# A product split over the chunks, a scaling moved to ScalarE, and additions moved from GpSimd to VectorE in a one-core decoder step

## The chip, the cores and the metric

The kernel runs on one core of a Trainium2 chip. The time is device microseconds of that core. Below, PE is the matrix engine TensorE (PEld its weight loads), DVE is VectorE, ACT is ScalarE, POOL is GpSimd, SP is SyncE, which issues transfers. PSUM is the memory that matrix products are summed in.

## The reference

One step of a decoder layer over 1032 tokens: a prompt of 1024 and 8 single sample tokens. All operands are float32.

```
h = rmsnorm(x)
u, v, z, xBC, dt = split(h @ w_in)             # one product, columns by part
a = u * (tril(W_s) @ layernorm(v) + b)         # gated mixing inside chunks of 128 tokens
xBC = silu(causal_conv(xBC, width 4));  dt = softplus(dt + bias)
y = ssd_chunked(x, dt, A, B, C)                # state-space scan, decays exp(dt * A)
x = x + concat(a, gated_norm(y, z)) @ w_out
k, v = rmsnorm(mem) @ w_k, w_v                 # 256 memory tokens, 4 heads
x = x + softmax((rmsnorm(x) @ w_q) k^T) v @ w_o
x = x + (silu(n @ w_gate) * (n @ w_up)) @ w_down,  n = rmsnorm(x)
return rmsnorm(x), the states and caches
```

## The kernel before

**Tiles.** Activations lie transposed: 128 features on the partitions, tokens along the row. The tokens go in three chunks, `CH = (0, 512), (512, 768), (768, 1032)`, so a product over one chunk has 512, 256 or 264 columns; `X[0]`, `X[1]`, `X[2]` are the scaled input of the three. Each weight panel is a 128x1024 tile. Every large product is made in three passes for precision: each operand is split into a high part (a cast by ACT, lines 145 and 274, tiles `wh`, `xh`, `fw`, `sP`) and the remainder (a subtraction by DVE or POOL, lines 146 and 275, tiles `wl`, `xl`), and PE adds high·high, high·low and low·high (`mm3`, line 169).

**Order.** One core, six queues; each engine runs its instructions in order. The order is made when the kernel is built, by a scheduler that walks the program and puts the instructions of the engines into their queues by a model of their times. Two other things set it: program order, and `later(n, work)`, which puts a piece of work into the program when `n` further matmuls have been issued (`mm3` counts them).

```
def later(n, work):
    queue.append([n, work])
```

**PSUM.** Products take a buffer from one of two pools: `gbank` (3 buffers, tiles named `g_...`) and `mbank` (5 buffers, `m_...`). A product whose pool has no free buffer waits for an evacuation.

**Stages in order.** Memory keys and values (`g_k`, `g_v`); scaling of the input into `X` (DVE line 383 writes `xtmp`, ACT casts `xh`, DVE or POOL subtracts `xl`); the dt product (lines 461 to 465, tiles `g_dt`), 16 columns of `w_in` split into `wd`, each chunk's 16 matmuls in a buffer of `gbank`; its transposes (`m_dtt`) and the decays (lines 505 to 569); the product that gives x, B and C (`xbc`, 8 panels, evacuated by `conv`, lines 586 to 596: ACT copies `cr` and writes `XS`, DVE adds the taps); the scan and the mixing; the queries (`qa`, `qb`); the attention, in which `scores` (line 1024) makes `ex`, `probs` transposes it (`m_pt`, split to `pTh` and `pTl`) and `pv` multiplies by the values (`m_pv`); the output projections `xoa` and `xob`, whose evacuation `norm_evac` (line 906 and on) adds to the residual `H`, squares it (`n3sq`, ACT) and sums the squares (`n3acc`, line 914); and the gate and up products.

**The gate.** Panels are multiplied in seven products a pair (P1 to P7, tiles `gX`, `gY`, `gZ`, `uX` ...), the sums and differences of two raw panels `fr` being made first (`ws`, lines 1227 to 1230, four of 128x512 a pair), then split into `fw`. The items `n` = 0, 1, 2, ... are gate and up in turn: the first two for one half of the columns alone (256 wide), the next two for both (256 and 264 wide). The norm before it ends late: for each chunk the sums of `n3acc` go through a product with ones (`m_csn`), a square root on ACT (`rsbn`), a few tiny DVE operations (`rsan`, `crvn`), and a product (`m_crn`) whose result scales `H` into `B` (DVE line 1174), which is then split into `sP`.

## Time and profile before

| | us |
|---|---|
| median of 3 runs | 1447.44 (1444.37 to 1452.41) |
| profiled execution, own time | 1451.7 |
| its span, first to last instruction | 1449.9 |
| PE busy | 1384.5 (95%) |
| DVE busy | 991.1 (68%) |
| ACT busy | 609.1 (42%) |
| POOL busy | 426.8 (29%) |

The profiled execution lies near the upper end of the runs. PE is busy almost throughout, so the places that matter are those where it waits (65 us of idle time in all) or runs at a lower granted clock: the row of the page that shows the clock in 40 slices of 36 us stands at 9 or below its full mark in all slices, and only windows of a few us show where it falls. The granted clock is given as a share of full speed: 1.00 is 2.4 GHz, 0.50 is 1.2 GHz, and a value between is a mixture of the two over the window.

### The profile page before, as it was taken

The page shows a single profiled execution, that of the slowest core. Times are in us where ns is not written, and L with a number is a line of the kernel's source. Part 1 is how long each engine was busy: PE and PEld are TensorE (multiplying, and loading weights), DVE is VectorE, ACT ScalarE, POOL GpSimd, SP SyncE. Part 2 cuts the span into 40 slices and gives each one's busy share as a digit, 9 for nine tenths or more (in the row PEclk, how much of TensorE's full clock was granted, in tenths as well). Part 3 has the DMA queues.
Part 4 walks back from the last instruction along what each step waited for, and adds up shares of the span by engine and source line. Part 5 has one row for each costly group of instructions (what it writes and reads, how often), then busy time and mean ns, then how long its engine had stood idle before and what let it go on. Part 6 is the DMA issues. An engine that isn't in the chain of part 4 may idle for free. (4 is left out here: it accounts for less than half of the span.)

```text
span 1449.9 us, 26101 instructions
## 1 busy us (share of the span) xinstructions
PE 1384.5 (95%) x10291; PEld 1313.1 (91%) x10291; DVE 991.1 (68%) x2018; ACT 609.1 (42%) x1103; POOL 426.8 (29%) x324
## 2 busy tenths in 40 slices
...
GB/s 292 195 60 60 61 145 114 99 60 36 217 162 74 175 268 285 88 271 250 148 88 129 169 141 149 118 126 168 154 157 212 169 181 302 222 178 165 204 195 131
DMA packets 145531, 232.67 MB, mean 160 GB/s; under 512 B 8328, under 2 KB 91880, under 8 KB 145024
## 3 DMA queue, kind: packets, MB, share of 16 engines
...
q10 hardware_dynamic: 144, 0.05, 0.0%
...
## 5 line engine op out<-in xcount | busy, mean ns | idle before, releaser
L275 DVE TENSOR_TENSOR fw<-ws,fw 128x512 fp32r<-128x512 f32 x96 | 90.0, 939 | 45.0 <-ACT fw L274 44.7
L145 ACT CAST wh<-wr 128x1024 fp32r<-128x1024 f32 (+1 forms) x85 | 87.9, 1037 | 75.5 <-PE g_gv L169 25.1
L274 ACT CAST fw<-ws 128x512 fp32r<-128x512 f32 x96 | 59.0, 619 | 137.7 <-POOL ws L1228 66.9
L146 POOL TENSOR_TENSOR wl<-wr,wh 128x1024 fp32r<-128x1024 f32 (+1 forms) x30 | 72.6, 2420 | 118.1 <-ACT wh L145 70.2
L1227 POOL TENSOR_TENSOR ws<-fr 128x512 f32<-128x512 f32 x24 | 35.9, 1498 | 210.7 <-DMA fr<-in_w_gate_dram 110.7
L146 DVE TENSOR_TENSOR wl<-wr,wh 128x1024 fp32r<-128x1024 f32 x55 | 71.1, 1295 | 24.7 <-ACT wh L145 24.6
L274 ACT CAST fw<-fr 128x512 fp32r<-128x512 f32 x72 | 44.4, 618 | 82.8 <-PE m_gY L169 20.6
L275 DVE TENSOR_TENSOR fw<-fr,fw 128x512 fp32r<-128x512 f32 x72 | 63.3, 879 | 8.3 <-ACT fw L274 7.9
L275 DVE TENSOR_TENSOR xP<-xsP,xP 128x512 fp32r<-128x512 f32 (+2 forms) x84 | 54.2, 686 | 14.9 <-ACT xP L274 13.4
L1532 PE MATMUL m_d<-xP,dwhi 128*128 128x264 f32 x448 | 64.1, 285 | 0.0
L275 DVE TENSOR_TENSOR dwlo<-dw,dwhi 128x1024 fp32r<-128x1024 f32 x32 | 39.8, 1244 | 34.0 <-ACT dwhi L274 33.9
L1532 PE MATMUL g_d<-xP,dwhi 128*128 128x256 f32 x448 | 63.0, 283 | 0.0
L169 PE MATMUL g_gY<-sP,fw 128*128 128x256 f32 (+1 forms) x432 | 59.1, 286 | 3.8 <-DVE t L1282 2.1
L169 PE MATMUL m_uY<-sP,fw 128*128 128x264 f32 (+1 forms) x432 | 58.5, 284 | 1.9 <-DVE fw L275 1.5
L169 PEld LDWEIGHTS g_gY<-sP,fw 128*128 128x128 f32 x432 | 54.9, 192 | 4.6 <-DVE t L1282 2.6
L1532 PEld LDWEIGHTS m_d<-xP,dwhi 128*128 128x128 f32 x448 | 58.5, 189 | 0.0
L1532 PEld LDWEIGHTS g_d<-xP,dwhi 128*128 128x128 f32 x448 | 57.7, 191 | 0.0
L169 PEld LDWEIGHTS m_uY<-sP,fw 128*128 128x128 f32 x432 | 54.6, 189 | 2.6 <-DVE fw L275 1.7
L274 ACT CAST xP<-xsP 128x512 fp32r<-128x512 f32 (+2 forms) x84 | 45.2, 588 | 27.2 <-DMA xsP<-x_d 17.4
L169 PE MATMUL m_gY<-sP,fw 128*128 128x264 f32 x360 | 49.4, 286 | 5.6 <-DVE t L1282 4.9
L274 ACT CAST dwhi<-dw 128x1024 fp32r<-128x1024 f32 x32 | 33.6, 1050 | 45.9 <-PE m_d L1532 36.4
L169 PEld LDWEIGHTS m_gY<-sP,fw 128*128 128x128 f32 x360 | 45.5, 188 | 7.1 <-DVE t L1282 6.1
(514 smaller groups left out, 3961.0 us busy)
## 6 DMA issues: line engine op xcount, KB each, us to landing
...
```

The source lines that it names most:

```text
L145: nc.scalar.copy(hi[:, s], r[:, s])
L146: (nc.gpsimd if i == 0 or P_QA <= i < P_XO[1] or P_XO[1] <= i < P_XO[1] + 8 and i % 2 else nc.vector).tensor_tensor(lo[:, s], r[:, s], f(h ...
L169: ins = nc.tensor.matmul(ps, lhs(k)[a], rhs(k)[b], start=(fresh and i == 0), stop=(i == n - 1), skip_group_check=not (fresh and done))
L274: nc.scalar.copy(dst_hi, src)
L275: (eng or nc.vector).tensor_tensor(dst_lo, src, f(dst_hi), op=ALU.subtract)
L1227: nc.gpsimd.tensor_tensor(s1, a21, a22, op=ALU.add)
L1532: nc.tensor.matmul(ps[:, : WQ[q]], wdn[n](k)[a], x_at(nm, q, k)[b], start=(i == 0), stop=(i == 3 * NPAIR - 1))
```

## The change

It has three parts. The dt product becomes a function `dt_product(ci)` of one chunk, in a buffer of `mbank`; it is called for the first chunk ahead of the x, B, C product, and for the other two, and for the decays, with `later`, 64, 100 and 120 matmuls into that product. In `scores` the exponentials are scaled by the reciprocal of their sum on ACT where it was DVE. And three pieces of GpSimd's work go to DVE: the remainders of every other panel of the second output projection's weights (4 of 128x1024), the sums of squares before the gate for panels 1 to 5 in each chunk (15 additions), and the panel sums of the first four gate and up items (16 of 128x512).

```diff
+LAG_D = (64, 100, 120)
...
-            (nc.gpsimd if i == 0 or P_QA <= i < P_XO[1] or P_XO[1] <= i < P_XO[1] + 8 and i % 2 else nc.vector).tensor_tensor(lo[:, s], r[:, s], f(hi[:, s]), op=ALU.subtract)
+            (nc.gpsimd if i == 0 or P_QA <= i < P_XO[1] else nc.vector).tensor_tensor(lo[:, s], r[:, s], f(hi[:, s]), op=ALU.subtract)
...
-        for ci in range(3):
-            w = CH[ci][1] - CH[ci][0]
-            ps = gbank(f"dt{ci}")
-            for i in range(16):
-                nc.tensor.matmul(ps[0:16, :w], wd[:, i % 8, :], X[ci](i % 8)[i // 8], start=(i == 0), stop=(i == 15))
-            nc.scalar.copy(dT[:, CH[ci][0] : CH[ci][1]], ps[0:16, :w])
...
+        def dt_product(ci):
+            w = CH[ci][1] - CH[ci][0]
+            ps = mbank(f"dt{ci}")
+            for i in range(16):
+                nc.tensor.matmul(ps[0:16, :w], wd[:, i % 8, :], X[ci](i % 8)[i // 8], start=(i == 0), stop=(i == 15))
+            nc.scalar.copy(dT[:, CH[ci][0] : CH[ci][1]], ps[0:16, :w])
+
+        def decays():
...
+        dt_product(0)
+        for n, work in zip(LAG_D, (lambda: dt_product(1), lambda: dt_product(2), decays)):
+            later(n, work)
         stage(plan_of(P_XBC, 8), X, conv, name="xbc")
...
-                    eng = nc.gpsimd if j < 6 else nc.vector
+                    eng = nc.gpsimd if j < 6 and nm == "n1" else nc.vector
...
-            nc.vector.tensor_scalar(ex[:, 0, :], ex[:, 0, :], sm[:, 0:1], None, op0=ALU.mult)
+            nc.scalar.activation(ex[:, 0, :], ex[:, 0, :], AF.Copy, scale=sm[:, 0:1])
...
             if nm == "P6":
+                eng = nc.vector if n < 4 else nc.gpsimd
                 s1, s2, s3, s4 = wsum[n] = [n3.tile([P, 512], F32, tag="ws", bufs=4, name=f"ws{n}_{i}") for i in range(4)]
-                nc.gpsimd.tensor_tensor(s1, a21, a22, op=ALU.add)
+                eng.tensor_tensor(s1, a21, a22, op=ALU.add)
```

The body of `decays` is what stood in lines 505 to 569, unchanged. In the pieces of order below, a name ends in the number of its tile (one number is one tile), the shape is that of the result, and x4 stands for four instructions of that kind in a row. The lines of the kernel after the change have numbers up to ten higher.

The first place is PE's queue around the dt product. Before, all 48 matmuls of the three chunks stand ahead of the first `g_xbc`; these are the last of them and what follows:

```order
L464 MATMUL g_dt_978<-xl_0_660,wd 16x256 x4
L464 MATMUL g_dt_978<-xl_1_661,wd 16x256 x4
L464 MATMUL g_dt_996<-xh_0_740,wd 16x264 x4
L464 MATMUL g_dt_996<-xh_1_741,wd 16x264 x4
L464 MATMUL g_dt_996<-xl_0_742,wd 16x264 x4
L464 MATMUL g_dt_996<-xl_1_743,wd 16x264 x4
L278 MATMUL m_dtt<-ident,dT 128x16 x4
L169 MATMUL g_xbc_0_1132<-xh_0_513,wh_885 128x512 x4
L169 MATMUL g_xbc_0_1132<-xh_1_514,wh_885 128x512 x4
L169 MATMUL g_xbc_0_1132<-xl_0_515,wh_885 128x512 x4
```

Here `g_xbc`, though it needs only the first chunk's `xh_0` and `xl_0`, comes after the third chunk's dt product, which needs `xh_2` and `xl_2` (written `xh_0_740` to `xl_1_743`). After the change the same place reads:

```order
L516 MATMUL m_dt_1006<-xl_1_516,wd 16x512 x4
L170 MATMUL g_xbc_0_1036<-xh_0_513,wh_885 128x512 x4
L170 MATMUL g_xbc_0_1036<-xh_1_514,wh_885 128x512 x4
L170 MATMUL g_xbc_0_1036<-xl_0_515,wh_885 128x512 x4
L170 MATMUL g_xbc_0_1036<-xl_1_516,wh_885 128x512 x4
L170 MATMUL g_xbc_0_1036<-xh_0_513,wl_886 128x512 x4
L170 MATMUL g_xbc_0_1036<-xh_1_514,wl_886 128x512 x4
L170 MATMUL g_xbc_0_1069<-xh_0_513,wh_1024 128x512 x4
...
L170 MATMUL g_xbc_1_1102<-xl_1_661,wh_885 128x256 x4
L516 MATMUL m_dt_1119<-xh_0_658,wd 16x256 x4
L516 MATMUL m_dt_1119<-xh_1_659,wd 16x256 x4
```

The first chunk's dt product is now followed at once by x, B, C for the first chunk of two panels (`g_xbc_0_1036` and `g_xbc_0_1069`); the second chunk's, `m_dt_1119`, has moved inside the first `g_xbc` of that chunk, and the third chunk's in the same way into the third.

The second place is the gate's beginning. In PE's queue before, from the first item's product P5 on, the norm products of the last two token parts (`m_csn_7853`, `m_crn_7891`, and earlier `m_csn_7725`, `m_crn_7762`) are spread between the first item's products:

```order
L169 MATMUL g_gZ_0_7967<-sP_7292,fw_7824 128x256 x10
L169 MATMUL g_gX_0_7830<-sP_7299,fw_7807 128x256 x2
L235 MATMUL m_csn_7853<-ones,n3acc_7358 128x1 x3
L169 MATMUL g_gX_0_7830<-sP_7299,fw_7807 128x256 x10
L169 MATMUL g_gZ_0_7967<-sP_7292,fw_7824 128x256 x2
L169 MATMUL g_gY_0_7880<-sP_7303,fw_7821 128x256 x12
L169 MATMUL g_gY_0_7880<-sP_7307,fw_7827 128x256 x12
L169 MATMUL g_gZ_0_7967<-sP3h_7310,fw_7844 128x256 x4
L169 MATMUL g_gZ_0_7967<-sP3l_7311,fw_7844 128x256 x4
L169 MATMUL g_gZ_0_7967<-sP3h_7310,fw_7844 128x256 x4
L278 MATMUL m_crn_0_7891<-ident,crvn_7857 128x128 x3
L169 MATMUL m_uX_0_8022<-sP_7288,fw_7877 128x256 x12
```

Between `m_csn_7853` and `m_crn_7891` stand 48 matmuls there. After the change PE's queue has, at the same place:

```order
L170 MATMUL g_gX_0_7830<-sP_7299,fw_7807 128x256 x12
L170 MATMUL g_gZ_0_7967<-sP_7292,fw_7824 128x256 x12
L236 MATMUL m_csn_7725<-ones,n3acc_7250 128x1 x2
L170 MATMUL g_gY_0_7880<-sP_7303,fw_7821 128x256 x12
L170 MATMUL g_gY_0_7880<-sP_7307,fw_7827 128x256 x12
L170 MATMUL g_gZ_0_7967<-sP3h_7310,fw_7844 128x256 x4
L170 MATMUL g_gZ_0_7967<-sP3l_7311,fw_7844 128x256 x4
L170 MATMUL g_gZ_0_7967<-sP3h_7310,fw_7844 128x256 x4
L279 MATMUL m_crn_0_7762<-ident,crvn_7728 128x128 x2
L236 MATMUL m_csn_7853<-ones,n3acc_7358 128x1 x3
L279 MATMUL m_crn_0_7891<-ident,crvn_7857 128x128 x3
L170 MATMUL m_uX_0_8022<-sP_7288,fw_7877 128x256 x12
```

Three of the four norm products have moved behind all of the first item's products, one directly behind another, ahead of the first up product `m_uX`. DVE's queue after the change holds this between `m_crn_7762`, which its first `B` row reads, and `crvn_7857`, which `m_crn_7891` reads:

```order
L276 TENSOR_TENSOR fw_7981<-ws_2_7958,fw_7981 128x512
L1183 SCALAR_TENSOR_TENSOR B_7765<-H_0_7004,vecT,m_crn_0_7762 128x256 x4
L1183 SCALAR_TENSOR_TENSOR B_7771<-H_1_7005,vecT,m_crn_0_7762 128x256 x4
L276 TENSOR_TENSOR fw_8019<-fr_1_7848,fw_8019 128x512
L220 TENSOR_SCALAR rsan_7858<-m_csn_7853 128x3
L221 RECIPROCAL crvn_7857<-rsbn_7859 128x3
L276 TENSOR_TENSOR sP_7906<-B_7765,sP_7905 128x1056
L222 TENSOR_TENSOR rsan_7858<-rsan_7858,crvn_7857 128x3
L223 TENSOR_TENSOR rsan_7858<-rsan_7858,rsbn_7859 128x3
L224 RECIPROCAL crvn_7857<-rsan_7858 128x3
```

The last operation of the norm's chain has moved behind the eight `B` rows, `fw_8019` and `sP_7906`. ACT's queue after the change, from the first `rsbn` on:

```order
L219 ACTIVATE rsbn_7730<-m_csn_7725,eps 128x2
L275 CAST fw_7964<-ws_1_7957 128x512
L275 CAST fw_7998<-ws_0_7956 128x512
L275 CAST fw_7981<-ws_2_7958 128x512
L275 CAST fw_8019<-fr_1_7848 128x512
L1302 ACT_TABLE_LOAD
L1302 ACTIVATE g_0_7799<-g_0_7799 128x2x256
L219 ACT_TABLE_LOAD
L219 ACTIVATE rsbn_7859<-m_csn_7853,eps 128x3
L1308 ACT_TABLE_LOAD
L1308 ACTIVATE g_0_7799<-g_0_7799 128x256
L275 CAST sP_7905<-B_7765 128x1056
```

The square root `rsbn` and the `Silu` of the gate now alternate, with a table load (`ACT_TABLE_LOAD`) at each turn, where before both `rsbn` stood ahead of the first `Silu` with one load; in the whole program the loads go from 29 to 35. The last row, `sP_7905`, is what `sP_7906` on DVE subtracts.

The third place is the attention. DVE's queue at its beginning before, with the scaling of `ex` in it (line 1030) among the reciprocals (`sm`) and the multiplications of the sample tokens' keys (`kc`):

```order
L1020 RECIPROCAL sm_0_5222<-sm_0_5222 128x1
L1030 TENSOR_SCALAR ex_0_5220<-ex_0_5220,sm_0_5222 128x256
L1020 RECIPROCAL sm_0_5253<-sm_0_5253 128x1
L1030 TENSOR_SCALAR ex_0_5251<-ex_0_5251,sm_0_5253 128x256
L1017 TENSOR_REDUCE mx_1_5297<-m_sc_1_5289 128x1
L991 SCALAR_TENSOR_TENSOR kc_0_5187,sdec<-kc_0_5187,qb_5185 128x256 x4
L991 SCALAR_TENSOR_TENSOR kc_1_5189,sdec<-kc_1_5189,qb_5185 128x256 x4
L1020 RECIPROCAL sm_1_5298<-sm_1_5298 128x1
L991 SCALAR_TENSOR_TENSOR kc_0_5193,sdec<-kc_0_5193,qb_5191 128x256 x4
L275 TENSOR_TENSOR pTl_0_5212<-m_pt_0_5304,pTh_0_5211 128x2x128
L991 SCALAR_TENSOR_TENSOR kc_1_5195,sdec<-kc_1_5195,qb_5191 128x256 x4
L1030 TENSOR_SCALAR ex_1_5296<-ex_1_5296,sm_1_5298 128x256
```

After the change DVE's queue there is:

```order
L1029 RECIPROCAL sm_0_5222<-sm_0_5222 128x1
L1029 RECIPROCAL sm_0_5253<-sm_0_5253 128x1
L1026 TENSOR_REDUCE mx_1_5297<-m_sc_1_5289 128x1
L1000 SCALAR_TENSOR_TENSOR kc_0_5187,sdec<-kc_0_5187,qb_5185 128x256 x4
L1000 SCALAR_TENSOR_TENSOR kc_1_5189,sdec<-kc_1_5189,qb_5185 128x256 x4
L1029 RECIPROCAL sm_1_5298<-sm_1_5298 128x1
L1000 SCALAR_TENSOR_TENSOR kc_0_5193,sdec<-kc_0_5193,qb_5191 128x256 x4
L1000 SCALAR_TENSOR_TENSOR kc_1_5195,sdec<-kc_1_5195,qb_5191 128x256 x4
L276 TENSOR_TENSOR pTl_0_5212<-m_pt_0_5304,pTh_0_5211 128x2x128
L1026 TENSOR_REDUCE mx_1_5355<-m_sc_1_5347 128x1
L276 TENSOR_TENSOR pTl_0_5212<-m_pt_0_5362,pTh_0_5211 128x2x128
L1029 RECIPROCAL sm_1_5356<-sm_1_5356 128x1
```

The scaling is gone from it. It stands in ACT's queue, as line 1039:

```order
L275 CAST pTh_0_5211<-m_pt_0_5304 128x2x128
L972 ACTIVATE Q_0_4856<-g_qa_0_5271 128x512
L1039 ACTIVATE ex_1_5296<-ex_1_5296,sm_1_5298 128x256
L275 CAST pTh_0_5211<-m_pt_0_5362 128x2x128
L1028 ACTIVATE ex_1_5354,sm_1_5356<-m_sc_1_5347,mx_1_5355 128x256
L1039 ACTIVATE ex_1_5354<-ex_1_5354,sm_1_5356 128x256
```

There `ex_1_5296` is scaled ahead of the next cast `pTh` and the next exponential, and needs `sm_1_5298`, which on DVE stands behind eight `kc` rows.

## Rows read from the trace of the kernel before

**Rows 1.** The page, part 1: busy us, share of the span, instructions.

```profile
PE 1384.5 (95%) x10291; PEld 1313.1 (91%) x10291; DVE 991.1 (68%) x2018; ACT 609.1 (42%) x1103; POOL 426.8 (29%) x324
```

**Rows 2.** PE's timeline, 70 to 100 us: start us, us, what.

```profile
71.22 0.63 PE L464 MATMUL g_dt<-xh,wd 128*16 128x256 f32 x4
...
87.00 2.90 PE L169 MATMUL g_xbc<-xh,wh 128*128 128x512 f32 x8
...
94.31 1.98 PE L169 MATMUL g_xbc<-xh,wh 128*128 128x512 f32 x8
...
99.75 0.52 PE L169 MATMUL g_xbc<-xh,wh 128*128 128x256 f32 x3
```

**Rows 3.** PE's waits, 60 to 112 us: total us, times, longest us.

```profile
PE g_dt L464 <- ACT xh L274: 6.6, 9, 3.0
```

**Rows 4.** Windows: length, busy PE, PEld, DVE, ACT, POOL, granted clock, DMA share, GB/s.

```profile
76.00:87.00 11.00, 7.81 (x30) 3.36 (x30) 7.59 (x19) 4.63 (x13) 5.29 (x7) 0.50 0.39 111
87.00:98.00 11.00, 11.00 (x47) 8.55 (x47) 4.57 (x16) 4.26 (x6) 0.00 (x0) 0.92 0.00 0
```

**Rows 5.** ACT's timeline, 70 to 108 us.

```profile
83.91 0.41 ACT L274 CAST xh<-xtmp 128x264 fp32r<-128x264 f32 x1 [0.51 <-DVE xtmp L383]
...
94.51 0.59 ACT L586 COPY cr<-g_xbc 128x512 f32<-128x512 f32 x1 [0.28 <-PE g_xbc L169]
95.00 0.79 ACT L587 ACTIVATE XS<-g_xbc,vecT 128x512 f32<-128x512 f32 x1
```

**Rows 6.** Line 1030 by itself: count, min/median/max ns, first and last start.

```profile
L1030 DVE TENSOR_SCALAR ex<-ex,sm x32: 332/354/2493, 514.5 to 670.4; 128x256 f32<-128x256 f32 x32
```

**Rows 7.** Line 419 by itself, the like operation on ACT.

```profile
L419 ACT ACTIVATE vt<-g_v,mrs x8: 461/467/475, 45.6 to 70.9; 128x256 f32<-128x256 f32 x8
```

**Rows 8.** DVE's timeline, 572 to 580 us.

```profile
576.96 2.49 DVE L1030 TENSOR_SCALAR ex<-ex,sm 128x256 f32<-128x256 f32 x1
```

**Rows 9.** POOL's timeline, 572 to 580 us.

```profile
576.92 2.38 POOL L146 TENSOR_TENSOR wl<-wr,wh 128x1024 fp32r<-128x1024 f32 x1 [0.67 <-ACT wh L145]
```

**Rows 10.** PE's waits, 500 to 690 us.

```profile
PE m_sc L169 <- DVE pTl L275: 3.7, 1, 3.7
PE m_pt L278 <- DVE sm L1020: 2.2, 1, 2.2
...
PE m_pt L278 <- DVE ex L1030: 1.7, 2, 1.3
```

**Rows 11.** Windows of the attention, DVE's densest stretch.

```profile
520.00:560.00 40.00, 36.71 (x190) 30.70 (x189) 36.10 (x145) 13.13 (x31) 10.97 (x5) 0.96 0.86 313
```

**Rows 12.** Windows from the output projection into the gate.

```profile
685.00:735.50 50.50, 48.14 (x396) 47.42 (x395) 42.39 (x59) 21.91 (x35) 29.98 (x20) 1.00 0.37 118
735.50:759.00 23.50, 20.64 (x149) 20.17 (x148) 21.90 (x47) 12.53 (x23) 7.66 (x4) 0.85 0.36 112
759.00:798.00 39.00, 34.22 (x275) 33.15 (x274) 38.73 (x51) 16.60 (x29) 17.20 (x10) 1.00 0.39 134
```

**Rows 13.** PE's waits, 685 to 798 us.

```profile
PE g_gY L169 <- DVE t L1282: 2.1, 1, 2.1
...
PE m_csn L235 <- DVE n3acc L914: 1.3, 1, 1.3
```

**Rows 14.** Line 275 by itself, 690 to 798 us.

```profile
L275 DVE TENSOR_TENSOR fw<-ws,fw x16: 672/686/1787, 734.0 to 796.1; 128x512 fp32r<-128x512 f32 x16
```

**Rows 15.** The tile n3acc by itself, 690 to 798 us.

```profile
L914 DVE TENSOR_TENSOR n3acc<-n3acc,n3sq x4: 433/498/569, 732.0 to 738.2; 128x256 f32<-128x256 f32 x2, 128x264 f32<-128x264 f32 x2
```

**Rows 16.** ACT's timeline, 730 to 770 us.

```profile
742.03 1.28 ACT L1278 ACT_TABLE_LOAD   x1
743.33 0.38 ACT L1278 ACTIVATE g<-g_gX 128x256 f32<-128x256 f32 x1
```

**Rows 17.** DVE's timeline, 735 to 768 us.

```profile
743.48 1.25 DVE L275 TENSOR_TENSOR sP<-B,sP 128x1056 fp32r<-128x1056 f32 x1
...
753.54 3.29 DVE L1174 SCALAR_TENSOR_TENSOR B<-H,vecT,m_crn 128x264 f32<-128x264 f32 x8 [0.22 <-PE m_crn L278]
```

More of the change, by code (lines that the diff above doesn't have):

```diff
@@ L515, in hymba_step @@
-        nc.vector.tensor_add(dtt, dtt, dtb.unsqueeze(1).broadcast_to([P, 9, NH]))
-        flat = dtt.rearrange("p c h -> p (c h)")
-        sp = w1.tile([P, 4, 72], F32, tag="ut", name="sp")
-        sp = [sp[:, i, :] for i in range(4)]
-        nc.vector.scalar_tensor_tensor(sp[0], flat, -1.0, flat, op0=ALU.mult, op1=ALU.min)
-        nc.scalar.activation(sp[0], sp[0], AF.Exp)
-        nc.vector.tensor_scalar(sp[1], sp[0], 2.0, None, op0=ALU.add)
-        nc.vector.reciprocal(sp[1], sp[1])
-        nc.vector.tensor_mul(sp[0], sp[0], sp[1])
```

97 lines of the change are left out of this document (53 added, 44 removed).

## The prediction

> **What bounds the kernel now.** I began with the page: PE is busy 95% of the span [rows 1], so only PE's waits and its stretches at a lower granted clock can be won, 65 us of waits in all. Then I read PE's waits, its timeline and the windows at each of the three places that the order changes. Ahead of x, B, C, PE's dt product waited nine times for ACT's cast `xh`, 6.6 us in all [rows 3], and from 76 to 87 us PE had a granted clock of 0.50 (1.2 GHz) [rows 4]. The first `g_xbc` started at 87.00 [rows 2], though its operands of the first chunk had been ready since the dt product's first part. In the attention PE waited for DVE's `pTl`, `sm` and `ex` [rows 10], and DVE was busy 36.1 of 40 us from 520 to 560 [rows 11]. From the output projection into the gate the reader is to see DVE's busy time against the window: 42.4 of 50.5, 21.9 of 23.5, 38.7 of 39 us [rows 12]. There DVE bounds, and PE waits for it [rows 13].
>
> A change of under 0.5% (7 us) can't be told from none here. The working is made against the profiled execution, 1451.7 us (its span is 1449.9); the median of the runs is 4.3 us lower, so the sum is taken off the median.
>
> **Part 1, the dt product: -13 us.** The first chunk's dt product ends where the second's begins, at 71.22 [rows 2]. After the change `g_xbc` stands next in PE's queue; its `X[0]` is the operand that the dt product has just read. So x, B, C begins 15.8 us earlier. What was there must still be paid: 32 dt matmuls of half width. Twenty-four 512-wide matmuls ran from 94.31 to 99.75 [rows 2], 0.227 us each at a granted clock of 1.00, so a half-wide one takes 0.113 and 32 take 3.6 us. The first eight `g_xbc` took 2.90 us, since PE came out of a stretch at 0.50, where eight at the full clock took 1.98 [rows 2]; with no gaps before them, 0.9 is won back. 15.8 - 3.6 + 0.9 = 13.1.
>
> What is late next? PE has chunk 0 of two panels first, 48 x 0.227 = 10.9 us, to 82.1. Chunk 1 follows; its X is cast well before that, and the third chunk's last cast ends at 83.91 + 0.41 = 84.3 [rows 5], needed only near 89. The narrow place is `gbank`, with three buffers: the fourth `g_xbc` needs one back. PE comes to it after 16 + 16 + 8 half-wide matmuls, 40 x 0.113 = 4.5 us, at 86.6. ACT frees the first buffer with `cr` (0.59) and `XS` (0.79) [rows 5], which stand in its queue after the last `xh` and the copy of `dT`: 84.3 + 0.4 + 0.6 + 0.8 = 86.1. That fits by half a microsecond, and every microsecond that ACT is late costs one. If ACT's evacuations fall behind by the two that queue there, about 4 us go: 9 to 14 is the range, 13 the value. The decays are the same instructions; their DVE and ACT work now lies beside the later panels, where it was partly before, and the scan that needs them comes some 80 us later. I cost that at nothing.
>
> **Part 2, the scaling on ACT: -3 us.** It takes 32 instructions from DVE, median 0.354 us and up to 2.493 [rows 6], and gives ACT 32 of the kind of line 419, 0.467 us [rows 7]: 32 x 0.47 = 15 us, where ACT was busy 13.1 of 40 us in the densest window [rows 11]. The long ones are those that stood beside a subtraction on POOL: one began at 576.96 and took 2.49 [rows 8], beside POOL's of 2.38 from 576.92 [rows 9]. PE's waits that hang on DVE there are 3.7, 2.2 and 1.7 us [rows 10]: 7.6 together, which is the most that can go. But the wait for `sm` stays, as the scaling now stands on ACT, for a reciprocal that stands on DVE behind eight `kc` rows; `pTh` and the next exponential are queued behind the scaling on ACT, and PE's transposes and scores wait for these. Twice the 2.2 us wait is my price for that: +4. DVE also gets the first chunk's five sums of squares and more weight remainders in this stretch. From -8 to +4; I take -3, nearer to the middle than to the full gain, as `ex` itself held PE for only 1.7.
>
> **Part 3, GpSimd's work on DVE: 0 us.** The additions on DVE, at the duration of the same shape without POOL beside it: 16 panel sums of 128x512 at 0.69 [rows 14], 11.0; 4 remainders of 128x1024 at 1.25, the nearest row [rows 17], 5.0; 5 sums of squares of 128x512 at 0.69 and 10 narrower ones at 0.43 [rows 15], 7.7. That is 23.7 us on an engine that was busy 103 of 113 us [rows 12]. Against it stands that its 157 instructions there ran long: `fw` took 0.67 to 1.79 us [rows 14], the long ones beside POOL. Taking each at its shortest, I estimate about 76 us of work, so 27 of the 103 us were lost beside POOL, and POOL is left with little. About 17 of the 24 us fall into these windows, so DVE would need 93 of 113: 38 of 50.5 in the first window, 23 of 23.5 in the second, 33 of 39 in the third.
>
> First window, where PE is idle for 50.5 - 48.1 = 2.4 us [rows 12]: the 1.3 us wait of `m_csn` for `n3acc` [rows 13] and some of the rest go, -2. Second: DVE is as full as it was, and here the order is worse. `m_crn_7891` stands on PE right behind `m_csn_7853`, and is held by DVE: from `m_crn_7762` on, eight `B` at 3.29 together [rows 17], `fw_8019` 0.69, `sP_7906` 1.25, three tiny ones, about 0.5: 5.7 us, less the 0.7 that PE spends on `m_csn_7853`. So PE stands for 5 us, where before 48 matmuls lay over that chain. The 2.1 us wait of `g_gY` for `t` [rows 13] goes in exchange, and with it the fall of the clock in that window, mean 0.85 [rows 12], though the new gap may bring it back. I take +3. Third: PE itself needs 34.2 of 39 us [rows 12], so at most 4.8 can go; the raw panels of the next item come free only when DVE's `fw` are done, so I take -1. Sum 0. The bounds are -8 (both waits and half of the third window's slack) and +9 (the chain twice as long, because ACT's four turns between square root and `Silu` lie on it).
>
> On these turns the row is plain: the load took 1.28 us and the next instruction began 0.02 us after its end [rows 16]. The Trainium skill ("ScalarE: Activation LUTs", section "What ACT_TABLE_LOAD costs") speaks against the change here: it gives 1283 ns for the load and some 1380 ns more for a drain, 2.66 us for every switch. For the two loads that lie inside the chain that would be an estimated 2.8 us more, and the forecast would be 1434. The trace shows the load and no drain behind it, so the sum does not hold it.
>
> **Sum.** -13 - 3 + 0 = -16: 1435.7 for an execution like the profiled one, and 1431.4 on the median; I say **1432**.
>
> **The rivals.**
>
> *POOL falls silent and DVE gains all of it.* If most of DVE's 27 us beside POOL come back at once, the gate's beginning is bound by PE, not by DVE: part 3 gives -8 instead of 0, and the time is 1423. For it: `fw` at 0.67 against 1.79 [rows 14]. Against it: PE has only about 10 us of waits from 685 to 798, and the new chain makes 5 of its own. The Trainium skill ("SBUF — State Buffer", section "Who interferes with whom") says that DVE with two inputs in SBUF and GpSimd reading SBUF exclude each other for whole instructions; by that rule all of the excess goes where POOL is idle, which is this rival.
>
> *New waits take the gain back.* Part 1 gives -13, the chain at the gate comes out at +9 by ACT's loads and casts in turn, and the attention at +4 because ACT's queue stands for reciprocals while DVE multiplies `kc`. That leaves 0: 1447, or 1443 with only the first of them. For it: the rows of order put the scaling ahead of `pTh`; DVE is at 36.1 of 40 us [rows 11]. Against it: 0.35 to 2.5 us leave DVE for each of these scalings [rows 6].
>
> *Nothing moves at x, B, C.* The product starts at 71 but stands for `gbank` or for the weights of its panels until about the old time, and part 1 gives under 3 us: 1444. Against it: both first panels' weights are among what was ready by 80 us, as PE ran 47 matmuls without a gap from 87 to 98 while no transfer ran (DMA share 0.00) [rows 4].
>
> *Slower: DVE's durations stay long.* If `fw` and the like are long by themselves in this stretch and not for POOL's sake, DVE has 103 + 23.7 = 127 us of work in 113. It is then the bound of all three windows, and the stretch grows by up to 24 us: 1447 - 13 - 3 + 24 = 1455. It decides from 16 us of growth on, two thirds of the added work. Against it: the same `fw` takes 0.67 and 1.79 in one window [rows 14], and the long scaling covers POOL's subtraction [rows 8, 9].
>
> **How the numbers follow.** The forecast, 1426 to 1438: 0.57. POOL silent, 1423: 0.13. New waits, 1443 to 1447: 0.18. Nothing moves, 1444: 0.05. Slower, 1455: 0.07. Eight in ten lie between 1420 and 1444: below it only the best of the first rival, above it the slower one and the end of the second. Faster by over 0.5% (below 1440.2) are the forecast, the first rival and a little of the second, 0.76; within, most of the second and third, 0.17; slower by over 0.5% the last, 0.07.
>
> **What would show it.** In the profile after: `g_xbc` begins near 71 us and no window up to 98 falls to 0.50; if it begins there but the first `XS` of ACT ends after 87, part 1 is smaller. In the attention no `ex` on DVE, ACT some 15 us busier, and PE's wait for `sm` turned into one for ACT's `ex`; a sum of waits over 12 us says that part 2 is wrong. At the gate, PE's longest wait is `m_crn` for `crvn`, about 5 us; `fw` on DVE lies near 0.69 throughout. If its median stays above 1 us with POOL idle, the slower rival holds.

## The result and the profile after

| | us |
|---|---|
| before, median | 1448.81 (1444.37 to 1452.41, 4 runs) |
| changed, median | 1430.85 (1427.07 to 1433.45, 4 runs) |
| ratio | 0.9879, 95% interval 0.9851 to 0.9906 |
| changed, profiled execution and its span | 1433.45, 1431.7 |

The change takes 18 us off (1448.81 - 1430.85); the prediction had 16. The profiled execution is 18.25 us shorter than the one of before. To see where that arose, the first or last matmul of each stage is set against the same one of before; the columns that the experiments need stand in a table of the same kind below. In the whole change PE is ahead by 15.2 us at the first `g_xbc`, 12.0 at the last, 11.8 at the queries' first `g_qa`, 15.0 at the first `g_xoa`, 14.8 at the first `g_xob`, 18.4 at the gate's first `g_gX`, and 16.7 at the first down product.

**x, B, C.** PE's timeline of the changed kernel at the dt product (start us, us, what), in answer to [rows 2]:

```profile
69.97 2.02 PE L516 MATMUL m_dt<-xl,wd 128*16 128x512 f32 x8
71.83 2.01 PE L170 MATMUL g_xbc<-xh,wh 128*128 128x512 f32 x8
...
84.63 1.10 PE L516 MATMUL m_dt<-xh,wd 128*16 128x256 f32 x8
...
88.01 1.23 PE L170 MATMUL g_xbc<-xh,wh 128*128 128x256 f32 x8 [0.40 <-ACT XS L592]
```

PE's waits from 60 to 112 us, in answer to [rows 3]:

```profile
PE g_xbc L170 <- ACT XS L592: 0.4, 1, 0.4
```

The windows there, columns as in [rows 4]:

```profile
76.00:87.00 11.00, 11.00 (x68) 9.47 (x67) 8.13 (x20) 5.63 (x13) 4.03 (x5) 1.00 0.36 120
87.00:98.00 11.00, 10.60 (x91) 9.79 (x90) 8.48 (x17) 9.01 (x18) 2.29 (x4) 1.00 0.09 26
```

The nine waits for `xh`, 6.6 us, are gone, and the granted clock is 1.00 where it was 0.50. A dt matmul of 256 columns now costs PE 0.12 us (the groups of eight start 0.94 apart); before, eight in a row took 1.93 us, 0.24 each, at a granted clock of 0.50, and most of those that read `xh` came one or two at a time with a wait between. One new wait is left, 0.40 us. It is at the place that the prediction called narrow; ACT's timeline shows what the fourth buffer of `gbank` had to wait for (in answer to [rows 5]):

```profile
76.48 1.05 ACT L146 CAST wh<-wr 128x1024 fp32r<-128x1024 f32 x1 [2.69 <-DMA wr<-in_w_in_dram]
...
85.91 0.41 ACT L275 CAST xh<-xtmp 128x264 fp32r<-128x264 f32 x1 [0.52 <-DVE xtmp L384]
86.23 0.57 ACT L517 COPY dT<-m_dt 16x512 f32<-16x512 f32 x1
86.71 0.57 ACT L591 COPY cr<-g_xbc 128x512 f32<-128x512 f32 x1
87.19 0.77 ACT L592 ACTIVATE XS<-g_xbc,vecT 128x512 f32<-128x512 f32 x1
```

The last `xh` comes 2 us later than before, at 85.91, so the evacuation ends at 87.96 and not at 86.1. The delay stands already at the cast `wh` ahead of these casts, which waited for its weights' transfer until 76.48, in before until 74.54.

**The attention.** The scaling by itself, on ACT, in answer to [rows 6, 7] (count, min/median/max ns, first and last start):

```profile
L1039 ACT ACTIVATE ex<-ex,sm x32: 495/510/554, 504.3 to 657.1; 128x256 f32<-128x256 f32 x32
its engine sat idle before it (us, times) until:
  DVE sm L1029: 8.3, 7
```

PE's waits from 485 to 675 us, in answer to [rows 10]:

```profile
PE m_pv L170 <- DVE pTl L276: 3.5, 3, 2.0
PE g_xoa L170 <- ACT ex L1028: 2.9, 1, 2.9
PE m_pt L279 <- ACT ex L1039: 2.6, 2, 2.2
PE m_pt L279 <- DVE pTl L276: 0.9, 1, 0.9
```

PE's transposes wait for the scaled `ex` on ACT (2.2 us the longest) as they waited for `sm` on DVE (2.2 us): ACT itself stood 8.3 us for the reciprocals. The long wait of `m_sc`, 3.7, is gone, and three of `m_pv` for `pTl`, 3.5 together, have come.

**The output projections and the gate.** The windows of the first and second output projection and of the 62 us after (columns as in [rows 4]):

```profile
596.90:670.80 73.90, 70.47 (x387) 60.20 (x386) 59.86 (x207) 34.91 (x87) 14.71 (x6) 0.95 0.71 250
670.80:718.10 47.30, 47.30 (x398) 47.30 (x397) 41.85 (x77) 21.91 (x34) 0.25 (x2) 1.00 0.44 131
718.10:780.10 62.00, 51.56 (x416) 50.89 (x415) 57.69 (x111) 34.55 (x56) 2.35 (x2) 0.94 0.36 121
```

The second projection was 50.9 us long, from the first `g_xob` at 685.6 to the first `g_gX` at 736.5, and is 47.3 now, without a wait of PE. POOL is empty in it. DVE's rows for line 276 over 675 to 785 us, in answer to [rows 14]:

```profile
L276 DVE TENSOR_TENSOR fw<-ws,fw x16: 676/692/1751, 715.8 to 777.3; 128x512 fp32r<-128x512 f32 x16
L276 DVE TENSOR_TENSOR fw<-fr,fw x13: 681/690/697, 710.6 to 779.5; 128x512 fp32r<-128x512 f32 x13
```

With POOL out of the way `fw` takes 0.69 us throughout, save one: the 1.75 began at 756.45, beside POOL's product `u` (1.29 us from 756.35). But PE's waits from 670 to 800 us are now (in answer to [rows 13]):

```profile
PE m_crn L279 <- DVE crvn L224: 8.0, 1, 8.0
PE g_gY L170 <- DVE t L1292: 1.3, 1, 1.3
PE g_gX L170 <- DVE fw L276: 1.1, 1, 1.1
```

DVE's timeline shows what `m_crn` waited for, after the previous norm product on PE had ended at 730.48:

```profile
731.20 0.69 DVE L276 TENSOR_TENSOR fw<-ws,fw 128x512 fp32r<-128x512 f32 x1
731.80 3.22 DVE L1183 SCALAR_TENSOR_TENSOR B<-H,vecT,m_crn 128x256 f32<-128x256 f32 x8
734.94 0.69 DVE L276 TENSOR_TENSOR fw<-fr,fw 128x512 fp32r<-128x512 f32 x1
...
737.20 1.26 DVE L276 TENSOR_TENSOR sP<-B,sP 128x1056 fp32r<-128x1056 f32 x1 [1.42 <-ACT sP L275]
...
738.76 0.18 DVE L224 RECIPROCAL crvn<-rsan 128x3 f32<-128x3 f32 x1
```

and ACT's what `sP` waited for, from the square root on (in answer to [rows 16]):

```profile
732.92 1.28 ACT L219 ACT_TABLE_LOAD   x1
734.22 0.26 ACT L219 ACTIVATE rsbn<-m_csn,eps 128x3 f32<-128x3 f32 x1
734.50 1.28 ACT L1308 ACT_TABLE_LOAD   x1
735.79 0.42 ACT L1308 ACTIVATE g<-g 128x256 f32<-128x256 f32 x1
736.12 1.05 ACT L275 CAST sP<-B 128x1056 fp32r<-128x1056 f32 x1
```

The five microseconds that the prediction gave to this chain are eight: DVE came to the first `B` 1.3 us late because of operations queued ahead, and then stood 1.42 us for ACT, whose two table loads lie on the chain. The instruction after a load begins 0.02 us after it, as before; there is no further time behind it. The gap also brought the lower clock back: the granted clock is 0.55 from 739.1 to 742.2, where the twelve matmuls of `m_uX` took 2.67 us and the twelve of `m_uY` behind them 1.60.

### The profile page after: what moved, and what is told of

It is laid out like the page before. It is cut to its first block, busy times and chain, and to the rows that moved or that the text cites. A ratio compares the mean times of both kernels' runs of the same rounds, so it can differ in the third digit from the quotient of the medians.

```text
span 1431.7 us, 26080 instructions
## 1 busy us (share of the span) xinstructions
PE 1373.5 (96%) x10291; PEld 1308.1 (91%) x10291; DVE 967.6 (68%) x2021; ACT 627.3 (44%) x1141; POOL 365.5 (26%) x289
## 5 line engine op out<-in xcount | busy, mean ns | idle before, releaser
L147 DVE TENSOR_TENSOR wl<-wr,wh 128x1024 fp32r<-128x1024 f32 x59 | 75.9, 1289 | 28.3 <-ACT wh L146 28.1
L147 POOL TENSOR_TENSOR wl<-wr,wh 128x1024 fp32r<-128x1024 f32 (+1 forms) x26 | 62.8, 2415 | 112.2 <-ACT wh L146 67.3
L1237 POOL TENSOR_TENSOR ws<-fr 128x512 f32<-128x512 f32 x20 | 26.8, 1341 | 200.4 <-DMA fr<-in_w_gate_dram 120.8
L276 DVE TENSOR_TENSOR fw<-fr,fw 128x512 fp32r<-128x512 f32 x72 | 59.5, 826 | 9.6 <-ACT fw L275 9.1
L276 DVE TENSOR_TENSOR xP<-xsP,xP 128x512 fp32r<-128x512 f32 (+2 forms) x84 | 55.0, 696 | 11.4 <-ACT xP L275 9.8
L1542 PEld LDWEIGHTS g_d<-xP,dwhi 128*128 128x128 f32 x448 | 57.7, 191 | 0.0
L1304 POOL TENSOR_TENSOR u<-u,g 128x512 f32<-128x512 f32 (+1 forms) x22 | 30.1, 1372 | 100.4 <-DVE u L1296 99.5
```

Source lines behind the costliest of these rows:

```text
L147: (nc.gpsimd if i == 0 or P_QA <= i < P_XO[1] else nc.vector).tensor_tensor(lo[:, s], r[:, s], f(hi[:, s]), op=ALU.subtract)
L276: (eng or nc.vector).tensor_tensor(dst_lo, src, f(dst_hi), op=ALU.subtract)
L1237: eng.tensor_tensor(s1, a21, a22, op=ALU.add)
L1304: nc.gpsimd.tensor_tensor(t, t, gates[q][:, 1, :, :], op=ALU.mult)
L1542: nc.tensor.matmul(ps[:, : WQ[q]], wdn[n](k)[a], x_at(nm, q, k)[b], start=(i == 0), stop=(i == 3 * NPAIR - 1))
```

## The experiments

Eleven kernels besides the whole change ran against before. Ratios are given with 95% intervals; a thousandth is 1.45 us. The first four take the parts singly and in one pair; the others ask what carries the third part, and one (10) what the scaling is worth inside the whole.

**1. The dt product alone.** The changed kernel with the scaling and all of GpSimd's work put back.

```diff
-            nc.scalar.activation(ex[:, 0, :], ex[:, 0, :], AF.Copy, scale=sm[:, 0:1])
+            nc.vector.tensor_scalar(ex[:, 0, :], ex[:, 0, :], sm[:, 0:1], None, op0=ALU.mult)
...
-                eng = nc.vector if n < 4 else nc.gpsimd
+                eng = nc.gpsimd
```

(and the other two choices of engine likewise put back)

> The dt product split over the chunks, alone; scaling on DVE and GpSimd's work on GpSimd as before. Theory: this part carries two thirds of the gain, -12 us (ratio 0.9917, between 0.989 and 0.994), all of it gained before the scan: g_xbc starts near 72 us, x, B, C ends 12 us earlier, and everything after runs as before. Rival (the split only looks early, the gain of the whole comes from GpSimd's silence): under -5 us, ratio above 0.9965.

Measured: 0.9924 (0.9903 to 0.9945), -11.0 us. PE is ahead by 14.5 us at the first `g_xbc` and 12.0 at the last. The theory holds, the rival falls.

**2. The scaling alone.** Before, with one line changed.

```diff
-            nc.vector.tensor_scalar(ex[:, 0, :], ex[:, 0, :], sm[:, 0:1], None, op0=ALU.mult)
+            nc.scalar.activation(ex[:, 0, :], ex[:, 0, :], AF.Copy, scale=sm[:, 0:1])
```

> The scaling of the exponentials on ACT, alone. Theory: -3 us, between -6 and +1 (ratio 0.996 to 1.001): the waits of PE for DVE's sm and ex become waits for ACT's ex, and the attention ends about 3 us earlier. Rival (DVE was what bound the attention): all 7.6 us of PE's waits for pTl, sm and ex go, ratio 0.995 or less. Other rival (ACT now stands for the reciprocals): +4 us.

Measured: 0.9979 (0.9965 to 0.9993), -3.0 us. PE's waits from 495 to 690 us:

```profile
PE m_pv L169 <- DVE pTl L275: 3.4, 3, 2.0
PE m_pt L278 <- DVE ol L275: 2.9, 1, 2.9
PE m_pt L278 <- ACT ex L1030: 2.4, 2, 2.0
```

As expected by the theory: a small gain, with PE waiting for ACT's `ex` and DVE's `pTl`. Both rivals lie outside the interval. The wait for `ol` is new; it returns in experiment 4.

**3. GpSimd's work on DVE alone.** Before, with the three engine choices of the change (that of the remainders is not shown).

```diff
...
-                    eng = nc.gpsimd if j < 6 else nc.vector
+                    eng = nc.gpsimd if j < 6 and nm == "n1" else nc.vector
...
+                eng = nc.vector if n < 4 else nc.gpsimd
...
```

> GpSimd's sums and remainders on DVE, alone. PE's order at the gate's beginning is the one of the whole change. Theory: near nothing, -2 us (ratio 0.996 to 1.002): the output projection gains 2 to 4 us, the first gate item loses 5 because m_crn waits some 8 us for crvn, the items behind it get 3 back. Rival (GpSimd's silence frees DVE): -8 us, ratio 0.9945 or less. Rival (DVE is overloaded): +7 us or more.

Measured: 0.9961 (0.9948 to 0.9974), -5.7 us: at the far edge of the theory's range, beyond its -2, and short of the first rival's -8. In its profile `m_crn` waits 8.0 us for `crvn`, as in the whole change, and the time is won all the same: 1.9 us in the first output projection, 3.6 in the second, and 0.5 between the gate's first and the first down product. So the size that I gave this part, nothing, was too small.

**4. The dt product and the scaling, without the third part.**

```diff
-                    eng = nc.gpsimd if j < 6 and nm == "n1" else nc.vector
+                    eng = nc.gpsimd if j < 6 else nc.vector
```

(and the other two choices likewise put back)

> The dt split and the scaling together, GpSimd's work left on GpSimd. Theory: the parts add up, -15 us (ratio 0.9895, between 0.987 and 0.992), within 3 us of the whole change; no long wait at m_crn, but DVE's fw of up to 1.8 us beside GpSimd. Rival (the third part is needed for the gain): at most -9 us, ratio above 0.9935.

Measured: 0.9918 (0.9893 to 0.9943), -11.9 us. The midpoint lies in the theory's range (0.987 to 0.992), at its far end, and not in the rival's (above 0.9935), though the interval reaches into both: that the two parts add up, to 14 by experiments 1 and 2, is not refuted. The theory's other half fails: the kernel is not within 3 us of the whole change (-18 us by the result, -22 by experiment 5's second reading), so the third part is needed for the rest. Beside experiment 1 the scaling added under 1 us, though the intervals overlap. The table shows where. Each number is the start of a stage's first matmul (for x, B, C the end of its last) against before, in us, from one execution each; before any of the changed places such numbers already differ by 1 to 2, so a difference of 2 in one cell is no evidence. The profiled execution of experiment 2 is the fastest of its ten (1441.56, their median 1447.38), so its column shows more than its runs do.

| stage | whole | 1 dt | 2 scale | 3 GpSimd | 4 dt, scale | 5 late m_crn | 6 no ws | 7 no squares | 8 no remainders | 9 remainders only |
|---|---|---|---|---|---|---|---|---|---|---|
| x, B, C end | -12.0 | -12.0 | -1.2 | -1.6 | -11.3 | -12.9 | -11.9 | -12.5 | -11.5 | -13.0 |
| g_qa | -11.8 | -13.9 | -2.6 | -1.6 | -11.2 | -13.1 | -11.6 | -13.2 | -13.7 | -13.0 |
| g_xoa | -15.0 | -14.5 | -6.4 | -1.3 | -15.8 | -17.6 | -16.3 | -17.4 | -18.4 | -16.8 |
| g_xob | -14.8 | -13.2 | -5.3 | -3.2 | -11.4 | -17.3 | -15.9 | -15.3 | -18.4 | -15.3 |
| g_gX | -18.4 | -12.0 | -5.3 | -6.8 | -11.4 | -20.9 | -19.5 | -18.9 | -22.0 | -15.1 |
| down | -16.7 | -9.8 | -9.1 | -7.3 | -10.6 | -21.8 | -18.3 | -18.8 | -22.5 | -13.2 |

In experiment 4 PE gains 4.6 us between the first `g_qa` and the first `g_xoa`, and loses them in the first output projection (-15.8 to -11.4). Most of that is a move and not a gain: with the scaling on ACT, 30 matmuls of the attention stand behind the first `g_xoa` that stood ahead of it. The first output projection in before has 357 matmuls and 67.6 us of PE, the whole change's above 387 and 70.5:

```profile
611.90:685.60 73.70, 67.56 (x357) 57.27 (x356) 65.19 (x203) 28.21 (x66) 24.04 (x12) 0.95 0.70 251
```

Experiment 4 has a wait of PE there besides:

```profile
PE m_pt L279 <- DVE ol L276: 3.0, 1, 3.0
```

This wait, 2.4 to 3.0 us, stands in the four kernels that have the scaling on ACT and the sums of squares on GpSimd (2, 4, 7 and 9) and in no other. So in the whole change the first projection holds (-15.0 to -14.8) in spite of the 30 matmuls, and the second gains 3.6.

**5. The chain at the gate hidden.** `m_crn` is issued 80 matmuls after its `m_csn`, where it was 20.

```diff
-                lagged_rstd(LAG_N, lambda rb: (use or normed)(ci, rb[0]), pool, [[acc[ci]]], ci, 1.0 / D, f"{nm}{ci}")
+                lagged_rstd((14, 80) if nm == "n3" and ci == 2 else LAG_N, lambda rb: (use or normed)(ci, rb[0]), pool, [[acc[ci]]], ci, 1.0 / D, f"{nm}{ci}")
```

> The whole change, with the last norm product m_crn (the one that waits 8.0 us for crvn) issued 80 matmuls after its m_csn where it was 20, so that it stands behind the up products of the first item. Theory: DVE bounds the gate's beginning (58.7 of 63.5 us busy over its first two windows), so most of the 8 us returns as a wait of the second half's products for sP: 0 to -3 us against the whole change, ratio 0.986 to 0.988. Rival (the order is what costs; PE stands for the chain): -5 us or more against the whole change, ratio 0.9845 or less.

The whole change, run once more in the same comparison:

> The whole change, once more beside the runs of before that the next three share. Both theories: ratio 0.988, between 0.986 and 0.990.

Measured: the whole change 0.9847 (0.9827 to 0.9867), with the late `m_crn` 0.9861 (0.9842 to 0.9880). No gain to be told; the 5 us that the rival expected against the whole change do not appear. PE's waits of the late `m_crn` from 714 to 780 us:

```profile
PE m_uX L170 <- ACT t L1283: 3.9, 1, 3.9
PE g_gY L170 <- DVE t L1292: 1.3, 1, 1.3
PE g_gY L170 <- DVE fw L276: 1.0, 1, 1.0
PE m_crn L279 <- DVE crvn L224: 0.8, 1, 0.8
```

The 8.0 us are 0.8, and the first up product `m_uX` starts 24.8 us ahead of before instead of 13.5; but `m_gX`, which needs the second half's `sP`, is ahead by 17.4 only, against 12.3 in the whole change. So a lead of 11.3 us over the whole change is 5.1 us within one item, and 2.5 of these stood already at `g_gX`. Part of it goes in a wait for ACT's copy `t`. The longest wait of the stretch was nearly worthless. What bounds the beginning is then most likely DVE's queue, 57.7 of 62 us busy in the whole change; that is argued from the busy time, and no run shows it by itself.

**6 and 7. The third part without one of its pieces:** the panel sums (6), the sums of squares (7) back on GpSimd.

```diff
-                eng = nc.vector if n < 4 else nc.gpsimd
+                eng = nc.gpsimd
```

```diff
-                    eng = nc.gpsimd if j < 6 and nm == "n1" else nc.vector
+                    eng = nc.gpsimd if j < 6 else nc.vector
```

> The whole change with the sums of panels (ws) back on GpSimd; sums of squares and remainders stay on DVE. Theory: the ws are the part that frees DVE at the gate (its fw beside GpSimd take 1.8 us instead of 0.69), so 3 to 5 us are lost against the whole change, ratio 0.990 to 0.9915. Rival (DVE was overloaded by them and the first item pays): -2 us against the whole change, ratio 0.9865 or less.

> The whole change with the 15 sums of squares before the gate back on GpSimd. Theory: they carry the gain of the output projection, 2 to 4 us, part of which comes back because PE's order at the gate then has seven groups of matmuls between the last m_csn and m_crn: +1 us against the whole change, ratio 0.988 to 0.9895. Rival (they carry none of it): the chain at the gate shortens and the whole gains, -3 us, ratio 0.986 or less.

Measured, in the comparison of 5: 0.9860 (0.9841 to 0.9879) without the panel sums, 0.9852 (0.9829 to 0.9874) without the sums of squares; the whole change had 0.9847. The loss that the theory expected of each does not appear. Both ratios lie in the range of the rivals, but the whole change came out lower here than expected as well, and against it there is no gain either: each piece can be taken back for nothing that can be told. These kernels differ from the whole change in PE's order too: `m_crn` waits 5.0 us in 6 and not at all in 7, where the whole change has 8.0, so each takes back a piece and part of a wait together. My next theory was that the third piece, the remainders, carries the gain.

**8 and 9. The whole without the remainders, and of the third part the remainders alone.** The edit of 8; experiment 9 has the two edits of 6 and 7.

```diff
-            (nc.gpsimd if i == 0 or P_QA <= i < P_XO[1] else nc.vector).tensor_tensor(lo[:, s], r[:, s], f(hi[:, s]), op=ALU.subtract)
+            (nc.gpsimd if i == 0 or P_QA <= i < P_XO[1] or P_XO[1] <= i < P_XO[1] + 8 and i % 2 else nc.vector).tensor_tensor(lo[:, s], r[:, s], f(hi[:, s]), op=ALU.subtract)
```

> The whole change with the remainders of every other panel of the second output projection (4 of 128x1024) back on GpSimd; sums of squares and ws stay on DVE. Theory: the third part's gain lies in the two output projections, and the remainders carry it: the second projection loses its 3.6 us again and the first some 2, +5 us against the whole change, ratio 0.9885 to 0.991. Rival (any two of the three pieces are enough, as the ws and the sums of squares each cost nothing when taken back): within 2 us of the whole, ratio 0.985 to 0.9875.

> The dt split, the scaling on ACT, and of GpSimd's work the remainders alone on DVE; ws and sums of squares on GpSimd. Theory (the remainders carry it): within 2 us of the whole change, ratio 0.985 to 0.988. Rival (it takes all three, GpSimd must fall silent): as without the third part, ratio 0.991 to 0.993.

Measured: 0.9857 (0.9843 to 0.9871) without the remainders, 0.9912 (0.9887 to 0.9937) with them alone. That theory falls too. The remainders alone do nothing that can be told (experiment 4 had 0.9918), and the other two without them do all. With the remainders on DVE it is enough that one of the other two leaves GpSimd (6 and 7); whether one is enough with the remainders on GpSimd was not run. The second projection's window of experiment 9 (columns as in [rows 4]):

```profile
670.20:721.40 51.20, 48.80 (x402) 48.38 (x402) 44.65 (x68) 22.88 (x36) 20.52 (x16) 0.99 0.42 133
```

This window falls into two groups. In before and in experiments 1, 2, 4 and 9 it is 50.9 to 52.1 us long, in all others 47.3, without a wait of PE. POOL works 20.5 us there in experiment 9 and 29.4 in before, but 7.5 without the panel sums, 13.1 without the sums of squares and 8.6 without the remainders. That looks like a threshold in POOL's work. But PE's order separates the two groups as well. In the long ones four matmuls of `m_csn` stand inside the last `g_xob` product, ahead of the first `g_gX`, and wait for `n3acc`, 1.3 us ([rows 13]) to 2.2; in the short ones they stand 9 to 48 matmuls behind the first `g_gX`, and nothing waits. PE in experiment 9:

```profile
718.58 0.58 PE L236 MATMUL m_csn<-ones,n3acc 128*128 128x1 f32 x4 [2.17 <-DVE n3acc L923]
...
721.37 2.66 PE L170 MATMUL g_gX<-sP,fw 128*128 128x256 f32 x12
```

PE, and the last addition that this `m_csn` reads on DVE, in the whole change:

```profile
718.06 1.59 PE L170 MATMUL g_gX<-sP,fw 128*128 128x256 f32 x12
...
723.81 0.50 PE L236 MATMUL m_csn<-ones,n3acc 128*128 128x1 f32 x4
```

```profile
719.44 0.43 DVE L923 TENSOR_TENSOR n3acc<-n3acc,n3sq 128x256 f32<-128x256 f32 x1
```

The sum was ready at 719.87 there, 1.8 us after the first `g_gX`; in experiment 9 at 718.43, 2.9 us ahead of it. So the wait did not go because the sum came earlier, but because its reader stands later. The scheduler chose that place when the kernel was built, and in every kernel here the place and POOL's load changed together: which of them a threshold belongs to is not shown. Of the 3.6 us, 2.4 are waits that went (1.3 for `n3acc`, 1.1 of `g_xob` for `H`) and 1.2 are less PE work in the window, of which the four matmuls, now in the gate, account for 0.4.

**10. The whole without the scaling.** The one line of experiment 2 put back.

```diff
-            nc.scalar.activation(ex[:, 0, :], ex[:, 0, :], AF.Copy, scale=sm[:, 0:1])
+            nc.vector.tensor_scalar(ex[:, 0, :], ex[:, 0, :], sm[:, 0:1], None, op0=ALU.mult)
```

> The whole change with the scaling of the exponentials back on DVE. Theory: the scaling on ACT is worth 3 us in the attention, ratio 0.988 to 0.9905. Rival (it only turns DVE's waits into ACT's): within 1.5 us of the whole change, ratio 0.985 to 0.9875.

Measured: 0.9873 (0.9859 to 0.9887), beside 0.9879 and 0.9847 of the whole. The scaling's worth inside the whole change is from nothing to some 4 us; the midpoint lies in the rival's range, but the interval does not tell the theory from the rival. PE's waits from 485 to 675 us sum to 12.5 us where the whole change has 10.4; the longest are:

```profile
PE m_pt L279 <- DVE ex L1039: 3.9, 3, 2.5
PE m_pt L279 <- DVE sm L1029: 2.4, 1, 2.4
PE g_xoa L170 <- ACT ex L1028: 1.9, 1, 1.9
PE m_pv L170 <- DVE pTl L276: 1.8, 2, 1.1
PE m_sc L170 <- DVE pTl L276: 1.5, 1, 1.5
```

The traces say a little more. From the first `g_qa` to the first `g_xob`, a stretch that holds the 30 matmuls in every kernel, PE gains on before 3.0 to 4.7 us in the six profiles that have the scaling on ACT and the sums of squares on DVE (the whole change twice, 5, 6, 8, 11), 1.6 and 2.0 with the sums of squares alone of these two (3, 10), and 0.2 to 2.7 with the scaling alone of them (2, 4, 7, 9); experiment 1, with neither, loses 0.8. That is about 2 us for each, from single executions.

**11. The late `m_crn` and the panel sums on GpSimd together.** The edits of 5 and 6.

```diff
+                lagged_rstd((14, 80) if nm == "n3" and ci == 2 else LAG_N, lambda rb: (use or normed)(ci, rb[0]), pool, [[acc[ci]]], ci, 1.0 / D, f"{nm}{ci}")
...
+                eng = nc.gpsimd
```

> The whole change with the late m_crn of 80 matmuls and with the ws on GpSimd, so that DVE has less to do at the gate's beginning. Theory (DVE's queue bounds the beginning, and both together shorten it): -3 us against the whole change, ratio 0.983 or less. Rival (GpSimd's ws slow DVE's fw by what they take from it): as each alone, ratio 0.985 to 0.9875.

Measured: 0.9849 (0.9837 to 0.9862), 1428.03 us. Its one profile has 3 us less than before between the gate's first and the first down product, but the runs do not show it against the whole change's 0.9847, from another comparison: the rival. No kernel here beats the whole change by what can be told.

## Why the prediction was right, and where its terms were off

The time, 1432 against 1430.85, is right, and so is the mechanism that carries it, the dt product. That the sum came within 2 us is partly luck: parts 1 and 2 were set too high and part 3 too low, by amounts that cancelled. The terms:

- *Part 1, -13.* Alone -11.0 (-7.9 to -14.0); in the trace 12.0 by the end of x, B, C. The start of `g_xbc` went as worked out (71.83 for 71.2), the dt matmuls cost what was set, and the narrow place at the fourth `gbank` buffer was where I put it, with 0.40 us of wait: the last `xh` came 2 us later than in before, and the margin of half a microsecond was gone. The mid-range value was 1 to 2 us too good.
- *Part 2, -3.* Alone -3.0, and by the mechanism named: PE's wait moved from `sm` to ACT's `ex`, ACT stood 8.3 us for reciprocals. In company less: beside the dt split it is under 1 us. What I had not seen is that the scaling also changes PE's order: 30 matmuls of the attention go behind the first `g_xoa`, so most of the lead there is a move, and with the sums of squares on GpSimd a wait for `ol` of up to 3.0 us comes as well. The 7.6 us that were called the most that can go left out a wait of 2.0 (`m_pt` for DVE's `pTl`, between the lines of [rows 10]); with it they are 9.6.
- *Part 3, 0.* This is the term that was mis-sized: it measured -5.7 alone, and from -11.9 (experiment 4) to some -20 (the whole, by its two readings) with the other parts. Window by window: second projection -3.6 for -2; the first item +4.9 for +3, because the chain at `m_crn` took 8.0 us and not 5 (DVE's operations ahead of `B`, ACT's table loads); the items after it -5.7 for -1 up to the first `g_uZ` (of which 0.5 to 2.5 came back before the down product, in the two profiles of the whole change). The gain of the second projection came with the move of `m_csn`, which the prediction did not weigh. I had weighed the other two as a cost and a small gain; experiment 5 says that they are one thing, since the time did not fall when the chain's wait went from 8.0 to 0.8. If DVE's queue was the bound of the whole stretch, as its busy time suggests, PE's stand for `crvn` only showed where PE met it, and adding the chain's price to DVE's work was counting a wait twice. DVE's work itself was set too low: the estimate that 27 of 103 us were lost beside POOL is too high, since the shortest duration of each form leaves some 18, and after the change DVE was busy 99.5 of 109.3 us from the first `g_xob` on, not 93 of 113. And the bound of -8 is not the sum that it names: 1.3 and 2.1 for the waits and 2.4 of slack are 5.8.
- *The rivals.* "POOL falls silent" is what happened to `fw`, 0.69 us save one; the part alone gave 6 and not 8, and gained more in the projections than in the gate. "Slower" falls with the same rows: the long `fw` were long for POOL's sake. "New waits" came where they were told, and were paid for by what they let go. The times given for it with one cost only, 1443, and for "nothing moves", 1444, leave out part 2's -3; with it they would be 1440 and 1441.

The rule of the Trainium skill on the table loads ("ScalarE: Activation LUTs", section "What ACT_TABLE_LOAD costs"), some 1380 ns of drain beyond the load, is not what these traces show: the square root after the load of 732.92 began 0.02 us behind its end. The Trainium skill's rule on the two engines that exclude each other ("SBUF — State Buffer", section "Who interferes with whom") is borne out: `fw` went from up to 1.79 us [rows 14] to 0.69 when POOL had nothing to do, and the one left at 1.75 stood beside POOL's `u`.

What stays open: the scaling's worth inside the whole change, which the traces put near 2 us and the runs between nothing and 4; and whether the third part pays by GpSimd's silence or by the order that the scheduler makes of it, since no run changed one without the other. Parts 2 and 3 without part 1 were not run together.
